# A pooling mixer on one core: S4 x B22 of the second input phase as seven inner products, its sums loaded, its stores on GpSimd's queue

## The chip, the core and the metric

The kernel runs on one core of a Trainium2 chip. Its engines work side by side, each through its own list of instructions in order, and wait for each other by semaphores: TensorE (PE: matmuls, with PEld for the loading of their stationary operand), VectorE (DVE), ScalarE (ACT), GpSimd (POOL) and SyncE (SP, which here only issues DMAs). A DMA that GpSimd issues runs in the software queue, one that SyncE issues in a hardware queue. The metric is the time of one execution on the device in microseconds (us). Three runs of the kernel before took 910.66, 911.06 and 911.10 us; the median is 911.06.

## The reference

The input x has 4096 rows (time) of 1024 channels. One layer of a pooling mixer is applied, with a norm before and a norm after:

```python
normed = rms_norm(x, norm_w)
u, gate = split(normed @ in_w, 2)               # in_w is 1024 x 2048
pooled[g] = trailing_mean(u[g], w_g) - u[g]     # 4 groups of 256 channels, w = 2, 4, 8, 16
mixed[g]  = pooled[g] @ group_w[g] + group_b[g]
y = mixed * scale * silu(gate)
out = rms_norm(x + y @ out_w, final_norm_w)
```

All of it is float32. What costs matmul time are the two large products, with in_w and with out_w.

## The kernel before, in words

**Precision.** Each operand of a matmul is split into a high part and a low part (`split`: ScalarE copies the high part, L165, VectorE subtracts for the low part, L159). A product is three matmuls: high x high, high x low, low x high.

**Weights.** group_w is multiplied into the u half of in_w at the start, so that an input product gives at once what is to be pooled.

**Stages.** The input product is made in two phases, a and b (`q` = 0 and 1), one for each two of the four groups: of its 1024 output columns, 512 are the gate and 512 are u. Each phase goes over NB = 4 blocks of 1024 rows. Then the output phase o goes over 8 blocks of 512 rows. In the trace, phase a runs from 33.8 to 324.7 us, the blocks of phase b begin at 324.7, 397.3, 469.8 and 542.3, and the output phase begins at 614.9 us.

**One block of an input phase.** It is a 2 x 2 block product by Winograd's form of Strassen's method, seven products in place of eight. A are the rows (split in two halves of time and two halves of channels), B the weights, C the result: C11 and C21 are gates, C12 and C22 are u. The products come in the order P1, P2, P7, P6, P5, P4, P3 (`ORDER_IN`), and each is one step:

- P1 = A11 B11, P2 = A12 B21, P4 = A22 by a combination of B;
- P7 takes S3 = A11 - A21, P6 takes S2 = A22 - S3, P5 takes S1 = A11 + S2;
- P3 = S4 B22 with S4 = A12 - S2; it is the last one, and completes C12.

A step is 48 matmuls (2 halves of channels x 4 tiles of columns x 2 x 3 passes) of a 128 x 128 stationary weight tile against 512 rows (`mm3`, L603). P1, P2, P7 and P4 collect in PSUM banks 0 to 3 (called x and v), P6, P5 and P3 in banks 4 to 7 (y). The sums of products are made by not clearing a bank between products, and by copying or adding banks on the way out (`evict_in`): P1's banks are copied to y; P2's go through Silu to C11 tiles; P6's and P7's are copied to tiles; P5's and P4's are added to those (L1033); P3's are copied.

**Sums.** In phase a, the operands A are read from a transposed x, normalized and summed (`form_in`), and the operands of P1, P2, P7 and P4 are also stored to DRAM (`sd`) through GpSimd's queue. Phase b loads those four back (`load_saved`, L532) and makes S2, S1 and S4 again (`form_in`, `form_s4`): six VectorE subtractions or additions of 128 x 1024 per block.

**Tiles.** Operands and results live in eleven `st` and eight `vt` tiles of 128 x 1024 floats, given out first in, first out (`Slots`): a tile comes free when its last reader is done, a store to DRAM among them. The split operands live in four `op` tiles, used in turn.

**Pooling.** When C21/C22 or C12/C11 are complete, `pool` makes the windowed sums on VectorE, multiplies by the gate, and stores the result to DRAM (`yd`, L792) by SyncE. `pool_later` says how many steps after its product this comes.

**Out weights.** In blocks 1 and 2 of phase b, after P5, `make_wo` loads rows of out_w, scales them on ScalarE (L246), combines them and stores the seven combinations (`wod`); block 3 loads and splits them (`load_w`).

**The output phase** multiplies what was stored in `yd` with these weights, again by seven products. From its third block on one of them, P2, is itself made as seven smaller products ("inner products", L701) with matmuls of 256 columns; their weights lie in four `st` tiles taken out of the turn (`kept`).

**Order.** The loop at the end of the kernel goes over all steps. At step n it issues the loads of the steps up to n + 3 (`load_reach`; n + 4 in phase o), the splits of step n + 1, the sums of step n + 2, the pooling that is due, and the product itself. A scheduler then orders each engine's instructions by these places in the program, except where `issue_after` holds an instruction behind a named one or `high_priority` moves it ahead. SyncE's queue and GpSimd's queue are in order: a DMA that waits holds up those behind it.

Of the kernel before, what the change touches and what calls it, by code (L numbers as in the profile page):

```python
# [15 lines left out]
P = 128  # L16
D = 1024
# [18 lines left out]
class Slots:  # L36
# [4 lines left out]
    def __init__(self, tiles):  # L41
        self.free = deque((0, t) for t in tiles)
        self.used = {}

# [9 lines left out]
    def keep(self):  # L54

        return self.renew(self.free.popleft()[1])

# [7 lines left out]
def kernel(  # L65
# [54 lines left out]

    def renew(t):
        i = next(i for i, u in enumerate(sts) if u is t)
        return mem.tile([P, D], F32R, tag=f"st{i}", name=f"inner{i}")

    st.renew = renew
# [41 lines left out]
    def split(dst, src):  # L167
# [17 lines left out]
        for i in range(P1, P7 + 1)  # L185
# [4 lines left out]
            for i in (P1, P2, P7, P4)  # L190
# [75 lines left out]
    def store_weights(dst, h, b11, b21, b12, b22):  # L266
        nc.sync.dma_start(out=dst[P1][h], in_=b11)
        nc.sync.dma_start(out=dst[P2][h], in_=b21)
        for i, u in combine(b11, b21, b12, b22).items():
            nc.sync.dma_start(out=dst[i][h], in_=u)  # L270
            give(u)

# [15 lines left out]

    def save_t3():

        for h in range(2):
            us = []
            for k in (h, 2 + h):
                us.append(take())
                nc.sync.dma_start(out=us[-1], in_=wvd[k])
            with tc.issue_after(evicted[0]):
                sub(us[0], us[1], us[0])
            nc.sync.dma_start(out=t3d[h], in_=us[0])
            for u in us:
                give(u)  # L300
# [22 lines left out]
    def split_wb(i):  # L323
        for h in range(2):
# [7 lines left out]
            if i != P6:  # L332
                give(u)

    def make_wo(h):
        us = {}
        for n in range(2):
            for kh in range(2):
                us[kh, n] = load_rows(out_w, 4 * kh + 2 * h, n * H)
                scale_rows(us[kh, n], pair(scale_c, h, kh))  # L340
        store_weights(wod, h, us[0, 0], us[1, 0], us[0, 1], us[1, 1])

    def load_w(src, i):
        for h in range(2):
            u = take()
            nc.sync.dma_start(out=u, in_=src[i][h])
            split(w[i][h], u)
            give(u)
# [187 lines left out]
    def load_in(q, b, i):  # L536
        s = xs[b]
        if i == P1:
            s["11"] = load_saved(b, P1) if q else load_x(b, 0, 0)
        elif i == P2:  # L540
            s["12"] = load_saved(b, P2) if q else load_x(b, 0, 1)
        elif i == P7:
            s["21"] = load_saved(b, P7) if q else load_x(b, 1, 0)
        elif i == P6:
            s["22"] = load_saved(b, P4) if q else load_x(b, 1, 1)

    def form_in(q, b, i):

        s = xs[b]
        if i in (P1, P2):  # L550
            if q == 0:
                for u in s["11" if i == P1 else "12"]:
                    normalize(b, 0, u)
        elif i == P7:
            if q == 0:
                for h in range(2):
                    normalize(b, 1, s["21"][h])
                    sub(s["21"][h], s["11"][h], s["21"][h])
        elif i == P6:
            s["2"] = [take(pool=early if (q, b) == (0, 0) else None) for _ in range(2)]  # L560
            for h in range(2):
                if q == 0:
                    normalize(b, 1, s["22"][h])
# [3 lines left out]
            if q == 0:  # L567
                give(rstd.pop(b))
        elif i == P5:
            for h in range(2):  # L570
                add(s["11"][h], s["2"][h], s["11"][h])
            if (q, b) != (0, 0):
# [3 lines left out]
    def split_in(q, b, i):  # L576
        s = xs[b]
        key = {P1: "11", P2: "12", P6: "2", P7: "21", P5: "11", P4: "22", P3: "12"}[i]
        later = q == 0 and b == 0 and i in (P1, P2)
        t = split_halves(s[key], None if q or later else sd[b].get(i))  # L580
        if later:
            stores.extend(zip(sd[0][i], s[key]))
        if i == P6 and (q or b):
# [24 lines left out]

# [839 lines left out]
```

## Time and profile before

| | before |
|---|---|
| median of three runs | 911.06 us |
| the profiled execution | 911.84 us |
| its span | 909.7 us |
| granted TensorE clock, mean | 0.997 |
| TensorE busy | 900.6 us (99%) |
| VectorE busy | 764.5 us (84%) |
| ScalarE busy | 461.8 us (51%) |
| moved by DMA | 178.08 MB, 196 GB/s on average |

The span goes from the first to the last instruction of the profiled execution; the 2.1 us beside it lie around it. Busy time is the time in which an engine had an instruction under way. Rows of groups read: line, engine, operation, written tile <- read tiles, shapes, x count | busy us, mean ns of one | idle time of the engine ahead of them <- what ended it. Rows of waits read: engine, line and who was waited for: us in total, times, longest. Rows of the chain read: start, us, what, count. Rows of DMA issues read: tiles, queue, count, KB each, us from issue to landing (the median).

### The profile page before, as it was taken

Reading aid. Unit: us, or ns where it says so; the run is one execution under the profiler, and the core shown is the slowest. Engines: PE = TensorE matmul, PEld = TensorE weight load, DVE = VectorE, ACT = ScalarE, POOL = GpSimd, SP = SyncE. Lnnn points to the kernel's source line nnn. Section 1 sums busy time; section 2 is a strip of 40 time slices with the busy share of each in tenths; the row PEclk is TensorE's granted clock in tenths of the full one; section 3 lists DMA queues with packets and bytes.
Section 4 is the critical chain, followed back from the end, with each engine's and each line's share of the span. In section 5 each row is a group of like instructions: output and inputs, shape, how many; then the busy total and the mean of one; then the engine's idle time right before and its main releaser. Section 6 shows DMA issues by size and latency. Waiting matters only on the chain.

```text
span 909.7 us, 11455 instructions
## 1 busy us (share of the span) xinstructions
PE 900.6 (99%) x4320; PEld 790.1 (87%) x4320; DVE 764.5 (84%) x909; ACT 461.8 (51%) x693; POOL 49.9 (5%) x124
## 2 busy tenths in 40 slices
PE   9999999999999999999999999999999999999997
PEld 7888888888888888888888888888888898888886
DVE  3889995985995997696798699699989878978886
ACT  7869547547446565355445545644424424335334
POOL 0020100100110000000000000000201001001000
PEclk9999999999999999999999999999999999999998
DMA  9977766577675454116616714636385464464332
GB/s 341 401 291 240 276 235 230 189 270 253 217 272 196 156 202 145 47 64 212 255 47 234 275 70 158 235 105 219 137 280 181 149 226 155 146 232 139 116 139 93
DMA packets 66807, 178.08 MB, mean 196 GB/s; under 512 B 6080, under 2 KB 23872, under 8 KB 66752
## 3 DMA queue, kind: packets, MB, share of 16 engines
q1 hardware_dynamic: 60176, 155.83, 48.8%
q0 software_dynamic: 5856, 20.46, 6.1%
q10 hardware_dynamic: 720, 1.06, 0.3%
q8 instruction: 34, 0.56, 0.2%
q14 instruction: 21, 0.17, 0.1%
HBM read 116.50 MB, written 60.83 MB: 195 GB/s over the span
## 4 chain that ended last, share of the span: by engine, by line
PE 91%; DMA 4%; DVE 3%; issue 1%; ACT 0%; SPq 0%; POOL 0%; DVEq 0%; ACTq 0%; POOLq 0%
PE bank L603 88%; PE bank L701 3%; DMA early<-in_wut 2%; DMA st<-in_x 1%; DMA vt<-yd 1%; DVE vt L1033 1%; PE bank L406 1%; DVE op L159 1%; DVE st L159 0%; DVE vt L916 0%; ACT st L943 0%; DVE vt L162 0%; DVE vt L711 0%; SPq L370 0%; DVE st L1033 0%
## 5 line engine op out<-in xcount | busy, mean ns | idle before, releaser
L603 PE MATMUL bank<-op,w 128*128 128x512 f32 x2688 | 580.9, 379 | 0.0
L603 PEld LDWEIGHTS bank<-op,w 128*128 128x128 f32 x2688 | 508.5, 189 | 71.8 <-ACT bank L165 0.4
L603 PE MATMUL bank<-w,op 128*128 128x512 f32 (+1 forms) x1212 | 262.2, 377 | 0.0
L603 PEld LDWEIGHTS bank<-w,op 128*128 128x128 f32 x1212 | 226.3, 189 | 30.7
L165 ACT ACTIVATE op<-st 128x1024 fp32r<-128x1024 f32 x129 | 134.7, 1053 | 142.2 <-PE bank L603 90.5
L159 DVE TENSOR_TENSOR op<-st,op 128x1024 fp32r<-128x1024 f32 x129 | 156.8, 1222 | 51.7 <-ACT op L165 51.3
L156 DVE TENSOR_TENSOR vt<-vt 128x1024 f32<-128x1024 f32 (+6 forms) x72 | 88.2, 1236 | 0.6
L159 DVE TENSOR_TENSOR op<-vt,op 128x1024 fp32r<-128x1024 f32 x43 | 52.5, 1222 | 19.8 <-ACT op L165 19.6
L165 ACT ACTIVATE vt<-bank 128x512 f32<-128x512 f32 x82 | 47.6, 593 | 41.4 <-PE bank L603 40.5
L165 ACT ACTIVATE op<-vt 128x1024 fp32r<-128x1024 f32 x43 | 45.1, 1053 | 39.3 <-PE bank L603 30.2
L159 DVE TENSOR_TENSOR st<-st,st 128x1024 f32<-128x1024 f32 (+1 forms) x43 | 47.0, 1111 | 2.3 <-ACT st L912 1.3
L165 ACT ACTIVATE bank<-bank 128x512 f32<-128x512 f32 x48 | 27.9, 581 | 32.9 <-PE bank L603 32.9
L1033 DVE TENSOR_TENSOR vt<-bank,vt 128x512 f32<-128x512 f32 (+1 forms) x55 | 37.1, 677 | 7.4 <-PE bank L603 7.0
L165 ACT ACTIVATE st<-bank 128x512 f32<-128x512 f32 x48 | 27.8, 593 | 28.7 <-PE bank L603 22.3
L207 POOL TENSOR_SCALAR oms<-oss 128x2 f32<-128x2 f32 x14 | 8.4, 601 | 565.5 <-ACT st L912 460.6
L159 DVE TENSOR_TENSOR w<-st,w 128x1024 fp32r<-128x1024 f32 x25 | 30.2, 1223 | 7.8 <-ACT w L165 7.8
L165 ACT ACTIVATE w<-st 128x1024 fp32r<-128x1024 f32 x25 | 26.0, 1052 | 14.2 <-PE bank L603 9.6
L788 DVE SCALAR_TENSOR_TENSOR st<-vt,colt,st 128x512 f32<-128x512 f32 x46 | 32.7, 752 | 0.1
L1033 DVE TENSOR_TENSOR st<-bank,st 128x512 f32<-128x512 f32 x42 | 28.8, 692 | 3.9 <-PE bank L603 3.7
L783 DVE SCALAR_TENSOR_TENSOR vt<-vt,vt 128x1024 f32<-128x1024 f32 x24 | 29.4, 1227 | 0.3
L916 DVE SCALAR_TENSOR_TENSOR vt<-vt,ors,st 128x1024 f32<-128x1024 f32 x18 | 22.5, 1282 | 7.9 <-POOL ors L225 7.9
L165 ACT ACTIVATE st<-st 128x1024 f32<-128x1024 f32 x16 | 16.9, 1059 | 21.8 <-DVE st L156 21.7
(132 smaller groups left out, 619.0 us busy)
## 6 DMA issues: line engine op xcount, KB each, us to landing
st<-in_x SPq DMA_DIRECT2D x30, 512.0 KB, 5.3
st<-in_xt SPq DMA_DIRECT2D x28, 512.0 KB, 5.6
sd<-st POOLq DMA_DIRECT2D x28, 512.0 KB, 4.6
vt<-in_x SPq DMA_DIRECT2D x27, 512.0 KB, 4.5
st<-sd SPq DMA_DIRECT2D x24, 512.0 KB, 4.2
yd<-st SPq DMA_DIRECT2D x23, 512.0 KB, 2.6
st<-yd SPq DMA_DIRECT2D x20, 512.0 KB, 4.6
out<-vt SPq DMA_DIRECT2D x18, 512.0 KB, 3.6
```

Source lines behind the costliest of these rows:

```text
L156: nc.vector.tensor_tensor(out=dst, in0=a, in1=b, op=ALU.add)
L159: return nc.vector.tensor_tensor(out=dst, in0=a, in1=b, op=ALU.subtract)
L165: return nc.scalar.activation(dst, src, func)
L207: (nc.vector if on_vector and not first else nc.gpsimd).tensor_scalar(out=ms, in0=ss, scalar1=1.0 / D, scalar2=EPS, op0=ALU.mult, op1=ALU.add)
L406: latest[0] = nc.tensor.matmul(ps, a[:, kk, 2 * j + t, :], maps, start=t + m == 0, stop=t == 1 and m == len(pairs) - 1,).ins
L603: latest[0] = nc.tensor.matmul(ps, a, b, start=start and n == 0, stop=stop and n == 2, skip_group_check=True).ins
L701: latest[0] = nc.tensor.matmul(ps, x1, x2, start=i in (P1, P7) and k + n == 0, stop=k == 1 and n == 2, skip_group_check=True,).ins
L783: nc.vector.scalar_tensor_tensor(out=s[:, :, at : at + H], in0=s[:, :, at : at + H], scalar=1.0 / win, in1=v[:, :, HIST:], op0=ALU.mult, o ...
L788: nc.vector.scalar_tensor_tensor(out=sg[:, j], in0=s[:, j, at : at + H], scalar=bias_c[2 * grp + j], in1=sg[:, j], op0=ALU.add, op1=ALU.mult,)
L916: nc.vector.scalar_tensor_tensor(out=us[j], in0=us[j], scalar=rs[:, j : j + 1], in1=fw[0], op0=ALU.mult, op1=ALU.mult,)
L1033: partial["added"] = nc.vector.tensor_tensor(out=dst, in0=src, in1=dst, op=ALU.add).ins
```

## The change

In phase b, for its blocks 0, 1 and 2 (`inner_at`):

1. P3 is made as seven inner products by the same method (`inner_in`): S4 and B22 are cut in 2 x 2 again, and each inner product is 12 matmuls with 256 columns, 84 in place of 48. Four half sums of S4 are made on VectorE and split (`split_inner_in`, `split_sums`); bank "one" is copied to "six" and "six" to "five" on ScalarE; VectorE adds the banks into the result (`to_rows`). The splits of the next step are issued in the middle of it (`then`).
2. The sums and low parts of the inner weights are made once, in block 0 (`form_inner_in`), and lie until the end of block 2 in four `st` tiles lent out of the turn (`lend`, `end`).

In both phases, for all blocks:

3. Phase a stores the operands of all seven products, phase b loads them all, and its `form_in` is gone.
4. In phase b the `yd` stores, and all `wod` stores, are issued by GpSimd in place of SyncE. `make_wo` is spread over three steps (load at P2, scale at P7, combine and store at P6); the loads and splits of the out weights in block 3 are two calls in place of one.
5. Most loads of phase b are issued two steps ahead in place of three. The splits of phase b from block 1 on have high priority. C21's and C22's pooling comes two steps after P4 where P3 is inner, and the Silu of C21 comes at the end of the inner step.
6. The raw operands of the t3 weights are loaded one step ahead of their subtraction, in block 3 of phase a in place of block 2.

```diff
+    def lend(self):
+
+        t = self.free.popleft()[1]
+        self.lent.append(self.index_of(t))
+        return self.renew(t)
+
+    def end(self):
+        for i in self.lent:
+            Slots.clock += 1
+            self.free.append((Slots.clock, self.revert(i)))
...
-            for i in (P1, P2, P7, P4)
+            for i in ORDER_IN
...
+        elif stage == 1:
+            with tc.issue_after(latest_copy[0]):
+                for (kh, n), u in wo_rows.items():
+                    scale_rows(u, pair(scale_c, h, kh))
+            nc.gpsimd.dma_start(out=wod[P1][h], in_=wo_rows[0, 0])
+            nc.gpsimd.dma_start(out=wod[P2][h], in_=wo_rows[1, 0])
+        else:
+            b11, b12, b21, b22 = (wo_rows.pop((kh, n)) for kh in range(2) for n in range(2))
+            with tc.issue_after(latest_split[0]):
+                us = combine(b11, b21, b12, b22)
+            for i, u in us.items():
+                nc.gpsimd.dma_start(out=wod[i][h], in_=u)
...
+        if q:
+            s[i] = load_saved(b, i)
...
+        if q:
+            t = split_halves(s[i])
+            if i == P3 and inner_at(b):
+                t = split_inner_in(t, s[i])
+            for u in s.pop(i):
+                give(u)
+            return t
...
+    def inner_at(b):
+        return b < NB - 1
...
+            sub(t3, b22, b12)
+            add(t2, t3, b11)
+            sub(t1, b22, t2)
+            sub(t4, b21, t2)
...
+        hi, lo = (st.lend().rearrange(pattern, **sizes) for _ in range(2))
+        copy(hi, r)
+        sub(lo, r, hi.bitcast(F32))
+        give(r)
...
+        (a11, a21), (a12, a22) = ([quarter(u, g) for g in range(2)] for u in us)
+        vs = [take("p (n k s a) -> p n k s a", n=2, k=2, s=2) for _ in range(2)]
+        (s4, s2), (s3, s1) = ([v[:, n] for n in range(2)] for v in vs)
+        sub(s3, a11, a21)
+        sub(s2, a22, s3)
+        sub(s4, a12, s2)
+        add(s1, s2, a11)
...
+        o = next_op("p (x n k s a) -> p x n k s a", x=2, n=2, k=2, s=2)
+        split(o, v)
+        give(v)
...
+            for ct in range(2):
+                bank, g = (y[place[0] + ct], place[1]) if place else (spare, ct)
+                ps = bank.rearrange("p (a s) -> p a s", s=2)[:, g * P : (g + 1) * P]
+                for k in range(2):
+                    lt = [v[:, k, ct * P : (ct + 1) * P] for v in b]
+                    r = [v[:, k].rearrange("p s a -> p a s") for v in t[i]]
+                    for n, (x1, x2) in enumerate(((lt[0], r[0]), (lt[0], r[1]), (lt[1], r[0]))):
+                        latest[0] = nc.tensor.matmul(
+                            ps, x1, x2, start=i in (P1, P7) and ct + k + n == 0,
+                            stop=k == 1 and n == 2, skip_group_check=True,
+                        ).ins
...
+        def to_rows(bank, *places):
+            src = bank.rearrange("p (c a s) -> p c s a", c=2, s=2)
+            for g, n in places:
+                dst = rows[n][:, :, HIST:].rearrange("p c (s a) -> p c s a", s=2)
+                dst = dst[:, :, :, g * P : (g + 1) * P]
+                add(dst, src, dst)
+
+        go(P1)
+        copy(six, one)
+        go(P2)
+        go(P4)
+        go(P6)
+        copied_on = copy(five, six).ins
+        then()
+        go(P3)
+        for c, dst in enumerate(cells(rows, HIST)):
+            with tc.issue_after(copied_on):
+                evicted[0] = copy(halved(dst), plain(y[c])).ins
+        to_rows(one, (0, 0))
+        to_rows(six, (1, 0))
+        go(P7)
+        to_rows(seven, (1, 0), (1, 1))
+        go(P5)
+        to_rows(five, (0, 1), (1, 1))
...
-            nc.sync.dma_start(
+            (nc.gpsimd if q else nc.sync).dma_start(
...
-            with tc.issue_after(evicted[0]) if i == P6 else nullcontext():
+            with ExitStack() as order:
+                if i == P6:
+                    order.enter_context(tc.issue_after(evicted[0]))
+                if kind == "b" and b:
+                    order.enter_context(tc.high_priority())
                 split_up[n] = split_in(kind == "b", b, i)
...
-            wait = int(b == 0) if kind == "a" else 1 if b < NB - 1 else 2
+            wait = int(b == 0) if kind == "a" else 2 if inner_at(b) else 1
...
+        early_one = b == 0 and i in (P1, P2, P7) or b == NB - 1 and i != P1
+        return 2 if kind == "b" and not early_one else 3
...
+        inside = kind == "b" and i == P3 and inner_at(b)
+        if inside:
+            for half in range(2):
+                split_sums(split_up[n], half)
+        else:
+            due()
```

More of the change, by code (lines that the diff above doesn't have):

```diff
@@ L804, in cells, with gates @@
         return [us[c // 2][:, c % 2, lo:] for c in range(4)]
+    def gates(us):
+        for u in us:
+            copy(u, u, AF.Silu)
     def evict_in(b, q, i, sets, seeds=4):
```

205 lines of the change are left out of this document (134 added, 71 removed).

## The prediction

> **What bounds the kernel now.** I read the page first (busy shares), then TensorE's waits, the chain that ended last, the engines by stretches, and last the groups by shape.
>
> ```profile
> span 909.7 us, 11455 instructions
> PE 900.6 (99%) x4320; PEld 790.1 (87%) x4320; DVE 764.5 (84%) x909; ACT 461.8 (51%) x693; POOL 49.9 (5%) x124
> PE bank L406 <- DMA early<-in_wut: 1.0, 3, 0.4
> PE bank L1135 <- PEq L1433: 0.8, 1, 0.8
> PE bank L406 <- DMA early<-in_group_w: 0.4, 1, 0.4
> PE bank L701 <- DVE vt L711: 0.3, 1, 0.3
> ```
>
> TensorE is busy for 99% of the span, and its whole list of waits is 2.5 us long: three rows of the first 30 us and 0.3 us late in the output phase. So the kernel lasts as long as its matmuls last, and an edit counts in two ways only: by the matmul time that it takes away, and by the waits that it puts between matmuls. Neither another engine's load nor a transfer's length is a term by itself.
>
> ```profile
> 47.57 655.54 PE bank L603 x3036
> 703.11 3.35 PE bank L701 x30
> 709.05 0.73 PE bank L701 x6
> 712.37 0.67 PE bank L701 x6
> 738.94 3.35 PE bank L701 x30
> ```
>
> In the chain, 3036 matmuls of 512 columns follow each other in 655.54 us: 215.9 ns each. The output phase already holds matmuls of 256 columns (L701, the same strided reading of the moving side, the same three passes); 30 take 3.35 us: 111.7 ns each. One stretch of six is at 121.7 ns (0.73 us), the next at 111.7.
>
> ```profile
> 252.20:324.70 72.50, 72.50 (x338) 63.56 (x337) 61.55 (x66) 37.79 (x55) 2.13 (x4) 1.00 0.59 201
> 324.70:397.30 72.60, 72.60 (x338) 63.65 (x337) 59.98 (x66) 34.68 (x47) 0.00 (x0) 1.00 0.33 115
> 397.30:469.80 72.50, 72.50 (x337) 63.56 (x337) 59.52 (x59) 34.54 (x52) 0.00 (x0) 1.00 0.45 167
> 469.80:542.30 72.50, 72.50 (x337) 63.56 (x337) 59.39 (x59) 34.37 (x52) 0.00 (x0) 1.00 0.51 182
> ```
>
> Columns: stretch, its length, then busy time of PE, PEld, DVE, ACT and POOL, clock, DMA share, GB/s. Rows 2 to 4 are blocks 0 to 2 of the second input phase. One is 72.5 us long, seven products of 10.36 us; the clock is full, VectorE has some 12.5 us free in it, ScalarE 38, the DMA engines half of their time. That is the room into which the change puts its work.
>
> **The sum, part by part.**
>
> *Inner products.* In three blocks P3 (48 matmuls of 512 columns) becomes seven products of 2 x 2 x 3 = 12 matmuls of 256: 84. 48 x 215.9 = 10.36 us, 84 x 111.7 = 9.38 us: 0.98 us less per block, 2.93 in all. The dear stretch (121.7 ns) would make it 10.22 us, 0.14 us less per block, 0.4 in all. I take 111.7, which both long stretches show. The Trainium skill ("TensorE: Matmul & The Clock Gate", section "Wait — 56ns, not 53.3ns?") gives a warm matmul its columns at 2.4 GHz and about 2.5 ns beside; as an estimate that is 109.2 ns for 256 columns, 9.17 us for 84, and 3.6 us less in all. The trace agrees at 512 columns and stands 2.5 ns above at 256, so the trace's figure decides.
>
> ```profile
> L159 DVE TENSOR_TENSOR op<-st,op 128x1024 fp32r<-128x1024 f32 x129 | 156.8, 1222 | 51.7 <-ACT op L165 51.3
> L165 ACT ACTIVATE op<-st 128x1024 fp32r<-128x1024 f32 x129 | 134.7, 1053 | 142.2 <-PE bank L603 90.5 <-DVE st L159 18.8 <-PE bank L701 11.3
> L159 DVE TENSOR_TENSOR st<-st,st 128x1024 f32<-128x1024 f32 x37 | 44.5, 1222 | 2.2 <-ACT st L912 1.3 <-ACT st L246 0.6 <-DMA st<-wvd 0.2
> L1033 DVE TENSOR_TENSOR vt<-bank,vt 128x512 f32<-128x512 f32 x53 | 36.2, 687 | 7.4 <-PE bank L603 7.0
> L165 ACT ACTIVATE bank<-bank 128x512 f32<-128x512 f32 x48 | 27.9, 581 | 32.9 <-PE bank L603 32.9
> ```
>
> *VectorE and ScalarE.* An inner block adds on VectorE four sums of half size (no such row; the nearest, 128x512 out of a bank, is 687 ns: 2.7 us), two low parts (1222: 2.4) and six adds out of the banks (687: 4.1): 9.3 us. The loaded sums take away form_in's six adds (1222: 7.3). Net +2.0 on 59.5, and block 0 pays another 5.2 once for the inner weights (4 x 0.69 + 2 x 1.22): 67.2 of 71.5 us at most, so not the bound. ScalarE gets two op copies (1053) and two bank copies (581) more: +3.3 on 34.5. Throughput costs nothing here; order can.
>
> *Order inside the inner step.* T is the end of P4, and the step lasts 9.38 us. By the instruction order and these durations, the copy of bank one to bank six, which P6 needs at T + 4.0 (36 matmuls after T), is done at T + 3.2; the copy of six to five, needed at T + 8.0, at T + 6.2; the next block's first operands, needed at T + 9.4, at T + 6.5. P4's last bank is drained by T + 0.8, and nothing writes there before. The thinnest slack is 0.8 us: no cost taken, 0.5 us per block as the other end.
>
> *Splits at higher priority.* They come earlier in both queues, not later. What stands behind them waits instead: pooling and gates, due a step or more later. Cost 0.
>
> ```profile
> SPq L792 <- DVE st L788: 168.6, 23, 21.0
> SPq L792 <- DVE vt L788: 46.6, 9, 11.1
> sd<-st POOLq DMA_DIRECT2D x28, 512.0 KB, 4.6
> st<-sd SPq DMA_DIRECT2D x24, 512.0 KB, 4.2
> yd<-st SPq DMA_DIRECT2D x23, 512.0 KB, 2.6
> st<-in_out_w SPq DMA_DIRECT2D x6, 512.0 KB, 5.3
> L515 POOL DMA_DIRECT2D sd<-st x25 | 13.4, 537 | 88.1 <-DVE tmp L162 36.3 <-DVE st L159 22.5 <-DVE st L162 18.9
> ```
>
> *Stores through GpSimd's queue.* Today SyncE stands for 215 us in front of yd stores (first two rows), and the loads behind a store wait with it. In the second phase these stores and the wod stores go to GpSimd, 0.54 us per issue on an engine that did nothing there. SyncE is freed, but the tile under a store comes free later (landing 4.6 us on GpSimd against 2.6 on SyncE), and a store may now stand behind another's wait on GpSimd. The Trainium skill ("DMA: Bandwidth & Descriptors", section "Anatomy of one DMA — SWDGE (gpsimd) path") gives such a DMA 2.0 us plus its bytes at 436 GB/s; for 512 KB that is an estimate of 3.2 us, 0.6 more than on SyncE, which the slacks below would take; by the trace's 4.6 it is 2.0 more, which they would not everywhere, and the trace decides. The price is in the tightest place, below.
>
> *Loads and saved sums.* 24 more stores in phase a and 24 more loads in b, 512 KB each: 3.1 MB per block on 14.6 (201 GB/s x 72.5 us) and on 8.3 to 13.2 MB; by the same rows the DMA share rises to about 0.72 in a3 and to 0.45 to 0.63 in b. The four tiles lent to the inner weights leave seven of eleven for b0 to b2, so a load there waits more often for a store.
>
> ```profile
> 33.80:107.10 73.30, 73.30 (x344) 64.08 (x344) 65.11 (x85) 56.67 (x87) 11.10 (x21) 1.00 0.78 290
> 69.00:72.00 3.00, 3.00 (x15) 2.63 (x15) 3.00 (x4) 3.00 (x5) 0.00 (x0) 1.00 1.02 418
> 72.00:75.00 3.00, 3.00 (x16) 2.63 (x15) 3.00 (x4) 3.00 (x7) 0.00 (x0) 1.00 0.22 86
> 74.48 0.57 ACT L165 ACTIVATE st<-bank 128x512 f32<-128x512 f32 x1
> 76.57 1.55 ACT L165 ACTIVATE st<-bank 128x512 f32<-128x512 f32 x3
> ```
>
> *Block 0 of phase a.* DMA is full (share 1.02) until 72 us, and the new P5 store is issued into that, by my count at about 66 us; ScalarE's eviction of 74.48 us now waits for its tile until the store has landed. P5 starts three steps before the block's end, at 76.0; its second bank is needed six matmuls later, at 77.3, and was free at 77.1 (the first of three evictions from 76.57). Landing between 70 and 75 us gives 0 to 1 us of waiting; I take 0.1.
>
> *The tightest place: block 1 of b, from P6 to P5.* u is the block's start, 397.3 in the trace of before.
>
> ```profile
> 434.31 1.04 ACT L165 ACTIVATE op<-st 128x1024 fp32r<-128x1024 f32 x1
> 436.38 0.60 ACT L165 ACTIVATE st<-bank 128x512 f32<-128x512 f32 x1 [0.54 <-PE bank L603]
> 438.97 0.60 ACT L165 ACTIVATE st<-bank 128x512 f32<-128x512 f32 x1 [0.70 <-PE bank L603]
> 439.46 1.05 ACT L165 ACTIVATE op<-st 128x1024 fp32r<-128x1024 f32 x1
> DMA to landing us min/median/max: 3.1/4.2/7.7
> DMA to landing us min/median/max: 2.9/3.8/10.2
> ```
>
> Before, P6's second bank was evicted at 436.38, ahead of P4's operand copies (439.46 on). In the changed order P4's first operand copy stands between the evictions of the first and the second bank, so a late load holds up the evictions, and P5 writes those banks. That load waits in SyncE's queue behind one whose tile comes free with P5's second low part (about u + 35.4 by my count of VectorE), and for a yd store on GpSimd that stands behind a wod store, which waits for a scaling, for a load of out_w and for the store before it. Issue at u + 36, landing at u + 40.2 (4.2 us: the first of the two landing rows, for loads of sd on SyncE in b), copy until 41.2, eviction until 41.8; P5 needs the bank at u + 42.7 (41.4 plus six matmuls). Slack 0.9 us. At 7.7 us the wait is 2.6. If the store at the chain's head lands like the slowest of sd on GpSimd (10.2, second landing row, 105 to 330 us) and not at 4.6, it is 4.7. I take 0, nearest to the medians; ends 0 and 4.7. In block 2 the same copy is ready at about u + 38, ahead of need.
>
> *Elsewhere.* The out weights in three stages, t3's loads ahead of their use and the later gates are the same instructions at other steps, 6 to 10 us from their users; where they stand in a queue ahead of a load is counted above. Cost 0. The output phase and the tail keep their order: 0 ± 0.3 us.
>
> Sum: -2.93 + 0.1 = -2.8 us. The profiled execution took 911.84 us, 2.1 beside its span; it would become 909.0. It stands 0.8 above the median of the runs, 911.06, so the median becomes **908.2 us**. Ends without the large waits: 907.5 (2.93, 0.4 for the scatter of the runs shown, 910.66 to 911.1, and 0.2 in the tail) to 909.2 (1 us of waits).
>
> **The rivals.**
>
> *Late operand in b1 (the opposite side).* For it: the order above, the long rows of SyncE's waits, seven tiles in place of eleven. Against: 0.9 us of slack at median landings, and DMA at 0.45 before. One landing of 7.7 us gives 2.6 - 2.8: 910.9 us, within 0.2%. From 4.7 us of wait on (the load lands 5.6 us later than I count) the kernel is slower by over 0.2%; that is 913.0, and with both stores of the chain at 10.2 (11.2 late, 10.3 of wait) 918.6.
>
> *The weights bound the small matmuls.*
>
> ```profile
> L701 PEld LDWEIGHTS bank<-inner,op 128*128 128x128 f32 x144 | 18.7, 192 | 1.6 <-DVE vt L711 1.1
> ```
>
> A weight load shows 192 ns, and 84 of them in a row would be 16.1 us, 5.8 more than P3 now in each block: 928.4 us. Against it stand the 30 matmuls in 3.35 us, which have a load each.
>
> *Phase a pays.* Where DMA is full the new stores push each other back. If the eviction of 74.48 comes at 77, P5 waits 2 us: 910.2 us, within 0.2%. Against: the share drops to 0.22 from 72 us on.
>
> *It does not shorten.* If the copy of one to six came 1.8 us later than I count in each block (0.8 of slack, then the 0.98), the saving would be spent: 911.1. Against: the output phase's own inner products (L701) wait 0.3 us in all.
>
> **How the numbers follow.** 0.2% (1.8 us) is about what a measurement of this kernel can tell from no change: 909.2 and 912.9 are the bounds. Forecast 0.64 (faster). Late operand 0.24: 0.12 small, 0.12 decisive. Phase a 0.06, no shortening 0.04 (both within). Weights 0.02. So faster 0.64, same 0.22, slower 0.14. The range leaves out the decisive late operand and the weights above (0.14) and about 0.05 below: 907.2 to 912.9. The forecast's own is 907.5 to 909.2.
>
> **What would show it.** Right: P3's steps of 9.4 us in b0 to b2, TensorE with no wait between 31 us and the output phase, matmuls of 256 columns at 112 ns, VectorE's busy time up by about 4 us over b (11.2 more, 7.3 less in b3), yd rows gone from SyncE's waits. Wrong: a wait of TensorE on a bank that ScalarE evicts, at P5 of b1 or of a0, with a load of sd as the copy's releaser; or 256-column stretches above 120 ns.

## The result, and the profile after

The changed kernel takes 924.11 us (median of six runs, 921.53 to 928.53) against 911.08 us before: a ratio of 1.0145, with a 95% interval of 1.0121 to 1.0168. It is 13 us slower, where 2.9 us faster was forecast. The profiled execution took 923.97 us, 12.1 us more than the profiled one before.

The page of the changed kernel, and the four longest of TensorE's waits:

```profile
span 922.2 us, 11888 instructions
PE 902.6 (98%) x4428; PEld 792.9 (86%) x4428; DVE 768.2 (83%) x927; ACT 469.1 (51%) x707; POOL 69.3 (8%) x176
PE bank L647 <- DVE op L177: 5.0, 2, 4.3
PE bank L731 <- DVE st L174: 3.4, 2, 2.6
PE bank L647 <- ACT st L183: 1.5, 2, 1.3
PE bank L647 <- DVE st L1196: 1.0, 1, 1.0
```

Four rows that were not there before hold 10.9 us, nearly all on VectorE. Where they lie shows the timeline of TensorE's matmuls (start, length, what, and in brackets the wait ahead of it; L731 is the inner product of phase b, L647 the old L603, L858 the old L701). The changed kernel:

```profile
386.63 2.84 PE L731 MATMUL bank<-op,w 128*128 128x256 f32 x24
396.00 42.90 PE L647 MATMUL bank<-op,w 128*128 128x512 f32 x198
440.23 19.69 PE L647 MATMUL bank<-op,w 128*128 128x512 f32 x90 [1.32 <-ACT st L183]
460.71 2.92 PE L731 MATMUL bank<-op,w 128*128 128x256 f32 x24 [0.79 <-DVE st L174]
470.17 62.33 PE L647 MATMUL bank<-op,w 128*128 128x512 f32 x288
535.11 4.35 PE L731 MATMUL bank<-op,w 128*128 128x256 f32 x24 [2.62 <-DVE st L174]
546.00 72.69 PE L647 MATMUL bank<-op,w 128*128 128x512 f32 x336
618.52 11.20 PE L647 MATMUL bank<-w,op 128*128 128x512 f32 x50
630.39 20.56 PE L647 MATMUL bank<-w,op 128*128 128x512 f32 x94 [0.67 <-DVE op L177]
651.99 11.59 PE L647 MATMUL bank<-w,op 128*128 128x512 f32 x51 [1.04 <-DVE st L1196]
667.92 47.87 PE L647 MATMUL bank<-w,op 128*128 128x512 f32 x213 [4.34 <-DVE op L177]
715.62 1.50 PE L858 MATMUL bank<-w,op 128*128 128x256 f32 x12
```

The same view of the kernel before:

```profile
614.89 88.22 PE L603 MATMUL bank<-w,op 128*128 128x512 f32 x408
702.95 1.50 PE L701 MATMUL bank<-w,op 128*128 128x256 f32 x12
```

With the block ends of before (397.3, 469.8, 542.3, 614.9) the distance between the two kernels at each boundary is:

| boundary | before | after | after - before |
|---|---|---|---|
| end of b0 | 397.3 | 396.0 | -1.3 |
| end of b1 | 469.8 | 470.2 | +0.4 |
| end of b2 | 542.3 | 546.0 | +3.7 |
| end of b3 | 614.9 | 618.5 | +3.6 |
| first inner product of the output phase | 702.95 | 715.62 | +12.7 |
| end of the span | 909.7 | 922.2 | +12.5 |

So block 0 gains, blocks 1 and 2 lose 1.7 and 3.3 us, and the first two output blocks, which the change hardly touches, lose 9 us.

What TensorE waited for in block 2, on VectorE, in the list of DMA issues and in GpSimd's timeline of the changed kernel:

```profile
524.29 0.69 DVE L177 TENSOR_TENSOR vt<-vt 128x512 f32<-128x512 f32 x1 [8.06 <-DMA wod<-vt]
wod<-vt POOLq DMA_DIRECT2D x10, 512.0 KB, 7.4
515.51 0.53 POOL L370 DMA_DIRECT2D wod<-vt  x1 [1.74 <-DVE vt L177]
```

The half sums of S4 are written to a `vt` tile whose last reader is a wod store. GpSimd issued it at 515.51; it landed 8.7 us later. VectorE stood still for 8.06 us, came late to the draining of P4's banks, and the first inner product waited 2.62 us for those.

In block 1 it was P4's operand, as the prediction's tightest place has it (1.32 us), and then the same draining (0.79 us), here behind a yd store on GpSimd: it was issued at 434.72 and landed 7.3 us later, SyncE's queue stood for it, and the loads of P3's operand went out only at 442.02. ScalarE's copy and VectorE's half sums came late behind them:

```profile
434.72 0.53 POOL L949 DMA_DIRECT2D yd<-st  x1 [4.43 <-DVE st L945]
448.42 1.06 ACT L183 ACTIVATE op<-st 128x1024 fp32r<-128x1024 f32 x1 [7.27 <-DMA st<-sd]
449.51 1.23 DVE L177 TENSOR_TENSOR op<-st,op 128x1024 fp32r<-128x1024 f32 x1 [8.56 <-ACT op L183]
```

The stretches around the output phase's beginning, columns as in the prediction (busy time of PE, PEld, DVE, ACT, POOL; clock, DMA share, GB/s); first before, its first two output blocks, then the changed kernel, its blocks 0 and 3 of phase b and the first output block:

```profile
614.90:650.00 35.10, 35.10 (x164) 30.78 (x163) 35.10 (x40) 9.67 (x13) 0.00 (x0) 1.00 0.53 182
650.00:686.00 36.00, 36.00 (x169) 31.55 (x168) 32.78 (x40) 18.46 (x28) 7.39 (x11) 1.00 0.62 218
```

```profile
324.80:396.00 71.20, 71.20 (x372) 63.50 (x371) 50.32 (x56) 37.83 (x52) 0.00 (x0) 1.00 0.40 140
546.00:618.50 72.50, 72.50 (x338) 63.51 (x337) 68.17 (x70) 39.66 (x56) 2.13 (x4) 1.00 0.63 212
618.50:655.50 37.00, 35.29 (x161) 30.00 (x160) 37.00 (x39) 9.59 (x11) 1.59 (x3) 1.00 0.50 155
```

Already before, VectorE was busy for 35.10 of the first output block's 35.10 us. Work that comes late into that stage can't be made up there. In the changed kernel block 0 has 9.7 us of VectorE's work less than before (50.32 against 59.98), block 3 has 4.0 more (68.17 against 64.18) although it lost 7.3 us of `form_in`, the sums that are now loaded.

One price was in no sum. After its two longest waits TensorE runs for some 3 us at half its clock (the value behind PE, PEld, DVE, ACT and POOL; stretches of the changed kernel):

```profile
532.00:535.10 3.10, 0.49 (x3) 0.10 (x2) 1.96 (x3) 1.81 (x4) 0.00 (x0) 0.94 0.00 0
535.10:538.10 3.00, 2.99 (x14) 3.00 (x15) 2.79 (x4) 0.53 (x2) 0.00 (x0) 0.50 0.00 0
667.90:671.00 3.10, 3.08 (x7) 2.52 (x8) 3.10 (x3) 0.00 (x0) 0.00 (x0) 0.50 0.98 342
```

The 24 matmuls at 535.11 took 4.35 us in place of 2.84, so the wait of 2.62 cost 1.5 more. Behind the wait of 1.32 us (440.23) 90 matmuls took 19.69 us, 219 ns each: no such loss.

### The profile page after: what moved, and what is told of

The parts are those of the page before. It is cut to its first block, busy times and chain, and to the rows that moved or that the text cites. A ratio compares the mean times of both kernels' runs of the same rounds, so it can differ in the third digit from the quotient of the medians.

```text
span 922.2 us, 11888 instructions
## 1 busy us (share of the span) xinstructions
PE 902.6 (98%) x4428; PEld 792.9 (86%) x4428; DVE 768.2 (83%) x927; ACT 469.1 (51%) x707; POOL 69.3 (8%) x176
## 5 line engine op out<-in xcount | busy, mean ns | idle before, releaser
L647 PE MATMUL bank<-op,w 128*128 128x512 f32 x2544 | 550.9, 379 | 1.5 <-ACT st L183 1.5
L647 PEld LDWEIGHTS bank<-op,w 128*128 128x128 f32 x2544 | 480.2, 189 | 70.7 <-ACT st L183 2.5
L647 PE MATMUL bank<-w,op 128*128 128x512 f32 (+1 forms) x1212 | 265.1, 379 | 6.1 <-DVE op L177 5.0
L647 PEld LDWEIGHTS bank<-w,op 128*128 128x128 f32 x1212 | 226.8, 190 | 39.2 <-DVE op L177 5.8
L177 DVE TENSOR_TENSOR op<-st,op 128x1024 fp32r<-128x1024 f32 x112 | 135.7, 1219 | 51.7 <-ACT op L183 51.3
L183 ACT ACTIVATE op<-st 128x1024 fp32r<-128x1024 f32 x112 | 117.0, 1053 | 116.0 <-PE bank L647 45.7
L183 ACT ACTIVATE op<-vt 128x1024 fp32r<-128x1024 f32 x66 | 69.2, 1055 | 78.0 <-PE bank L647 42.8
L177 DVE TENSOR_TENSOR op<-vt,op 128x1024 fp32r<-128x1024 f32 x66 | 80.1, 1218 | 13.3 <-ACT op L183 13.0
L174 DVE TENSOR_TENSOR vt<-bank,vt 128x512 f32<-128x512 f32 (+1 forms) x57 | 36.1, 677 | 3.8 <-ACT vt L183 2.0
L1196 DVE TENSOR_TENSOR vt<-bank,vt 128x512 f32<-128x512 f32 (+1 forms) x43 | 28.8, 670 | 6.6 <-PE bank L647 6.5
L551 POOL DMA_DIRECT2D sd<-st x38 | 20.3, 534 | 129.1 <-DVE tmp L180 35.1
L180 DVE TENSOR_TENSOR st<-st,vt 128x1024 f32<-128x1024 f32 x22 | 26.1, 1215 | 3.4 <-DMA vt<-rd 3.4
L1079 DVE SCALAR_TENSOR_TENSOR st<-st,ors,st 128x1024 f32<-128x1024 f32 x16 | 20.1, 1281 | 6.8 <-POOL ors L243 6.8
```

What stands on the lines that cost most here:

```text
L174: nc.vector.tensor_tensor(out=dst, in0=a, in1=b, op=ALU.add)
L177: return nc.vector.tensor_tensor(out=dst, in0=a, in1=b, op=ALU.subtract)
L180: nc.vector.tensor_tensor(out=dst, in0=a, in1=b, op=ALU.mult)
L183: return nc.scalar.activation(dst, src, func)
L551: first_saves.append(nc.gpsimd.dma_start(out=saved[h], in_=u).ins)
L647: latest[0] = nc.tensor.matmul(ps, a, b, start=start and n == 0, stop=stop and n == 2, skip_group_check=True).ins
```

## The experiments

All times are medians; each ratio is to the kernel before on the same chip, with its 95% interval. On the chips used the kernel before took 911.1 to 911.6 us, so times from two chips compare to about half a us. Waits are read from one profiled execution each; such an execution can lie up to 4.6 us from the median (e17). Theory A: the stores on GpSimd's queue hold tiles too long. Theory B: the inner products with seven tiles are too tight by themselves. After the first four runs came C (pooling one step later leaves VectorE behind at the output phase), D (the four tiles that the output phase keeps back, the `kept` tiles, taken half a block earlier than before, from P5 of output block 0 on; the list of the change ahead leaves this edit out) and E (out weights split one step later).

### Who issues the stores, and the inner products left out

```diff
 # e1: both edits; e2: only the second (three places)
-            (nc.gpsimd if q else nc.sync).dma_start(
+            nc.sync.dma_start(
-            nc.gpsimd.dma_start(out=wod[P1][h], in_=wo_rows[0, 0])
+            nc.sync.dma_start(out=wod[P1][h], in_=wo_rows[0, 0])
```

> The changed kernel with the yd and wod stores of the second phase issued by SyncE again; all else as changed. Theory A (the stores on GpSimd's queue land late, 5.8 us for wod and 4.8 for yd at the median, and the tiles under them hold up what takes them next: the inner half sums in block 2 waited 8.1 us for a wod store) expects VectorE's 8.1 us wait to go, TensorE's waits in phase b and in the output phase to fall from 12 to under 3 us, and 908 to 911 us. Theory B (seven tiles in place of eleven and the inner work are too tight by themselves, whoever issues the stores) expects waits of the same size in other places and 918 us or more.

Measured: 918.7 us, 1.0080 (1.0064 to 1.0097). TensorE's timeline:

```profile
388.84 2.84 PE L731 MATMUL bank<-op,w 128*128 128x256 f32 x24
460.38 2.84 PE L731 MATMUL bank<-op,w 128*128 128x256 f32 x24
531.92 2.84 PE L731 MATMUL bank<-op,w 128*128 128x256 f32 x24
664.60 47.93 PE L647 MATMUL bank<-w,op 128*128 128x512 f32 x213 [4.26 <-DVE op L177]
```

The inner steps now begin 71.54 us apart, where a block took 72.5: 0.97 us less, just the matmuls' saving, and no wait in phase b. So A is right for phase b: with the stores on SyncE the change earns its 2.9 us there. But the 4.3 us wait in the second output block stays (4.26). The forecast of A, 908 to 911, is missed by 8 us, and something else must cause that wait. The time is as B forecast (918 or more), but not at B's place: phase b has no wait with its seven tiles.

> The changed kernel with only the wod stores issued by SyncE again; yd stores stay on GpSimd. If the wod stores are the part of theory A that counts (block 2's 8.1 us wait, and the work of VectorE that it pushes into the output phase), 911 to 915 us, with the 4.3 us wait in the output phase gone. If the yd stores count as much, or theory B holds, 918 us or more.

Measured: 919.86 us, 1.0089 (1.0072 to 1.0105). The 8 us wait of VectorE is gone, and of TensorE's waits in phase b 1.0 us is left. The 4.34 us wait is still there, so it doesn't come from block 2's stall, against the expectation. The wod stores alone are 4.2 of the 5.4 us between the changed kernel and the one with all its stores on SyncE.

```diff
 # e3
     def inner_at(b):
-        return b < NB - 1
+        return False
```

> The changed kernel without the inner products: P3 is 48 matmuls in all blocks, no inner weights, no lent tiles; sums are still loaded, stores still on GpSimd, splits still at high priority. Theory A expects that it stays slow: 916 us or more (2.9 us of matmul time come back, and the late stores stay). Theory B expects 909 to 912 us: no wait of TensorE in phase b and none over 1 us in the output phase.

Measured: 914.21 us, 1.0032 (1.0020 to 1.0044), between the two expectations. Without inner products, but with stores on GpSimd, phase b has no wait, and the 4.3 us are gone; a wait of 2.08 us comes later, at 708 us. The inner products, which save 2.9 us of matmuls, cost 9.9 us in the changed kernel (924.11 less 914.21), together with what the edit takes out beside them: the four lent tiles and the pooling two steps after P4.

> The kernel before with one part alone: yd stores of the second phase and all wod stores on GpSimd's queue. Theory A expects 914 us or more, from tiles that come free late. Theory B expects 911 us, within 1 us, since eleven tiles give the stores time to land.

Measured: 913.03 us, 1.0019 (1.0010 to 1.0028), between the two expectations. Its edit is the same change of queue, made to the kernel before. One wait comes of it, and it lowers the clock behind it as well:

```profile
496.38 122.39 PE L603 MATMUL bank<-op,w 128*128 128x512 f32 x558 [2.00 <-ACT vt L165]
496.30:499.40 3.10, 3.02 (x8) 2.51 (x9) 2.09 (x2) 1.93 (x3) 0.48 (x1) 0.60 0.87 262
```

So the queue alone costs 1.5 us with eleven tiles and six adds per block, and 5.4 us in the changed kernel. A holds in kind, though less than it forecast.

### The wait in the second output block

In the run with the stores on SyncE, the operand that comes late at 664.60 is loaded by SyncE like this:

```profile
646.81 0.32 SPq L949 DMA_DIRECT2D yd<-st  x1
647.18 0.43 SPq L1012 DMA_DIRECT2D vt<-yd  x1
```

The load stands right behind a yd store, which waits for block 3's last pooling on VectorE. In the changed kernel the same load is issued at 650.12, when that pooling frees its tile. Both lead to VectorE's pooling and to the tiles; each of the next four runs is meant to take away one suspect. All are the kernel with its stores on SyncE (918.7 us) and one more edit.

```diff
 # e5: inner products in blocks 0 and 1
-        return b < NB - 1
+        return b < NB - 2
```

> The stores on SyncE (918.7 us), and the inner products in blocks 0 and 1 only, so that block 2's P4 half is pooled one step after P4 as before. Theory C (pooling one step later moves one half's pooling, about 14 us of VectorE, out of each block into the next, and the last one's into block 3 and the output phase, where VectorE has no room) expects the 6 us of TensorE's waits at 624 to 665 us to fall under 2 us: 910 to 912 us, 1 us of matmul time more included. Theory D (the four tiles kept back from output block 0 on, in place of block 1, make its loads late) and theory E (the out weights, split one step later, are late) expect 917 to 920 us.

Measured: 913.70 us, 1.0018 (1.0007 to 1.0029), between the expectations of C and of D and E. The wait fell from 4.3 to 1.63 us:

```profile
656.98 46.46 PE L647 MATMUL bank<-w,op 128*128 128x512 f32 x214 [1.63 <-DVE op L177]
```

Its runs stand in two groups, 911.1 to 911.3 (three, the profiled one among them) and 912.5 to 915.0 (seven). In the profiled one the clock held after a wait of 1.63 us. The mean granted clocks go with the groups: 0.998 to 0.999 in the three, 0.996 to 0.997 in six of the seven. That the clock fell behind this wait in those is likely, but no trace of them shows it.

```diff
 # e6: block 2's P4 half is not pooled
+            cut = q == 1 and b == 2 and half == 1
-            if win == 2:
+            if cut:
+                pass
+            elif win == 2:
...
-            for j in range(2):
+            for j in range(0 if cut else 2):
```

> The stores on SyncE (918.7 us), three blocks with inner products, and for block 2's P4 half the windowed sums, the mean and the product with the gate left out (the gate itself is stored): 7 adds of 1.24 us, 2 means of 1.22 and 4 products of 0.75, 14.2 us of VectorE less, at the same steps and with the same tiles and stores. Theory C expects the waits in the output phase under 2 us and 908 to 911 us. Theories D and E expect 916 us or more, since the tiles and weights come as before.

Measured: 911.82 us, 1.0004 (0.9994 to 1.0014). With 14.2 us of VectorE's work less the load goes out at 641.22 us in place of 647.18, the wait is 2.29 us (in a profiled execution of 914.33 us), and the kernel is as fast as before, though not faster; C's range is missed by 0.8 us, its limit for the wait by 0.3. VectorE's lateness is one cause; a wait remains that it doesn't explain.

```diff
 # e7: the tiles kept back as before
-        if kind == "o" and b < 2 and not inner_w and (b or i in (P5, P4, P3)):
+        if kind == "o" and b == 1 and len(kept) < 4 and not inner_w:
...
-            if len(kept) == 4 and b:
+            if len(kept) == 4:
```

> The stores on SyncE (918.7 us), and the four tiles of the output phase's inner weights kept back from output block 1 on, as in the kernel before. Theory D expects the 4.3 us wait at 664 us to go: 911 to 914 us. Theories C and E expect 917 to 920 us.

Measured: 913.32 us, 1.0022 (1.0013 to 1.0032), as D expected. In place of the long wait there are 1.04 and 0.61 us, and 0.88 us later, in the third output block. The fourth load of yd in the output phase, which went out at 647.18, goes out ahead of the store that waits for the pooling:

```profile
629.79 0.37 SPq L1012 DMA_DIRECT2D st<-yd  x1
```

> The stores on SyncE (918.7 us), and the out weights loaded and split in one call in block 3, as in the kernel before. Theory E expects the waits of 1.4 and 0.7 us at 626 us and the 4.3 us at 664 us to go: 910 to 913 us. Theories C and D expect 917 to 920 us, with at most the 2 us at 626 us gone.

Its edit calls load and split of the out weights together after each product of block 3, as the kernel before does. Measured: 915.78 us, 1.0044 (1.0029 to 1.0059). The waits near 626 us are 1.8 us in place of 2.0; the long one is 3.1, with 0.7 ahead of it. E is the smaller part: 2.9 of 7.2 us.

So the load is late because four tiles are missing (D) and because the pooling is late that would give others back. Taking away either one takes 5 to 7 us of the 7.2 by which that kernel stood above the one before (918.70 against 911.55). That the pooling is late because it comes one step later, as C has it, is not shown: e5 also takes block 2's inner work away and ends the loan of the four tiles a block earlier, and e6 leaves work out altogether.

### Together, and each alone

> The stores on SyncE, three blocks with inner products, and both small restorations together: four tiles kept back from output block 1 on, out weights loaded and split in one call. If the two act on different waits, their gains add: 918.7 - 5.4 - 2.9 = 910.4 us. If both only make room for the same late pooling (theory C), 912 to 914 us, with waits of TensorE on VectorE left in the output phase.

Measured (edits of e7 and e8 together): 912.96 us, 1.0016 (1.0006 to 1.0026). The gains don't add. TensorE's list of waits:

```profile
PE bank L654 <- DVE st L1203: 1.8, 1, 1.8
PE bank L654 <- DVE op L177: 1.5, 1, 1.5
PE bank L865 <- DVE vt L875: 0.9, 1, 0.9
```

4.2 us, all on VectorE, all in the first three output blocks. That is nearly the balance: the median is 1.8 us above before, and the matmuls save 2.9, which makes 4.7.

> The same two restorations with the yd and wod stores on GpSimd's queue, as in the change. If the stores' price (5.4 us between the changed kernel and the one with its stores on SyncE) is paid in blocks 1 and 2, by tiles that come free late, it stays: 4 to 7 us above the run with the stores on SyncE, and VectorE's wait for a wod store in block 2 is there. If it was paid through the output phase, within 1.5 us of that run.

Measured: 927.05 us, 1.0168 (1.0138 to 1.0197), 14.1 us above the run before it, which differs only in who issues the stores. Block 2's stall is there, 8.5 us of VectorE waiting for a wod store, and in the first output block one more wait, of TensorE (in a profiled execution of 922.81 us):

```profile
DVE vt L177 <- DMA wod<-vt: 8.5, 1, 8.5
631.40 1.15 PE L654 MATMUL bank<-w,op 128*128 128x512 f32 x2 [5.00 <-ACT op L183]
```

The expectation for a price paid in blocks 1 and 2 (4 to 7 us) is exceeded; the stall is carried on to where VectorE has no room, and grows there.

> The stores on SyncE, inner products in blocks 0 and 1 only, out weights loaded and split in one call. Theory C with the late weights as a second load on VectorE: 910 to 912.5 us, the 1.6 us wait at 657 us gone. If only the tiles count there (theory D), 913.7 us as without it, within 1 us.

Measured: 913.82 us, 1.0033 (1.0021 to 1.0046): no better than with two inner blocks alone (913.70), as theory D expected. Two waits of 1.6 us on VectorE, at 627 and 660 us.

> The stores on SyncE, inner products in blocks 0 and 1 only (913.7 us), and the splits of phase b without high priority. If the priority is what keeps the splits ahead of the pooling, TensorE waits in blocks 1 and 2 for split operands: 916 us or more. If it only reorders VectorE's work, within 1 us of 913.7.

Its edit takes the high priority away. Measured: 914.54 us, 1.0034 (1.0025 to 1.0044), 0.8 us above the run with it, where the two intervals overlap. One wait of 0.60 us in phase b: the priority is worth little either way.

> The changed kernel with inner products in blocks 0 and 1 only; stores on GpSimd and all else as changed. If pooling one step later in block 2 is what fills VectorE before the output phase, and block 2's half sums are what waits for the wod store, both go: 913 to 917 us, and VectorE's 8 us wait for a wod store is gone. If the stores on GpSimd cost as much without it, 920 us or more.

Measured: 917.78 us, 1.0066 (1.0046 to 1.0085). On the changed kernel itself, too, block 2 without inner products takes 6.3 us away. VectorE's 8 us wait for a wod store is gone, as expected (one of 0.8 us is left); waits of 2.53 us in block 1 and 1.50 in block 3 for evictions by ScalarE remain, and 1.33 and 2.38 us on VectorE in the output phase. The expected range is missed by 0.8 us.

> Three blocks with inner products and both restorations (912.96 us), with the yd stores of block 3 alone on GpSimd's queue. If what is left in the output phase comes from loads that stand behind those stores in SyncE's queue, 910 to 912 us and the waits at 625 and 708 us shorter. If it comes from VectorE's work alone, within 1 us of 913.

Its edit issues the yd stores of block 3 alone through GpSimd. Measured: 913.14 us, 1.0017 (1.0007 to 1.0027), with the same three waits (2.0, 1.2 and 0.9 us). So what is left doesn't come from block 3's stores in SyncE's queue; VectorE's work is the cause that fits.

> Stores on SyncE, inner products in blocks 0 and 1, the four tiles kept back from output block 1 on (with one free tile left over in place of two, without which they are not there in time). If the pooling and the tiles were the two causes in the output phase, both are gone: 909 to 911 us. If VectorE is still behind there, 913 to 914 us as with each alone.

Measured: 914.00 us, 1.0036 (1.0023 to 1.0048). Both causes reduced, and no gain: 1.45, 0.90 and 1.95 us of waits on VectorE, the last at 810 us. Neither expectation named that place.

> The changed kernel without inner products and with all stores on SyncE: what is left are the loaded sums, the splits at high priority, the out weights in stages and the tiles kept early. If the sums' extra traffic costs nothing and the rest is harmless without the inner products, 911 to 912 us. If the loaded sums cost by themselves, 913 us or more.

Measured: 915.40 us, 1.0046 (1.0031 to 1.0061). Phase b runs without a wait, so the loaded sums cost nothing there. But the late load is back, without any inner product and with block 2's pooling one step after P4 as before (in a profiled execution of 920.02 us, 4.6 above the median):

```profile
663.37 49.05 PE L645 MATMUL bank<-w,op 128*128 128x512 f32 x214 [4.56 <-DVE op L177]
```

With the stores on GpSimd and no inner products (914.21) it wasn't there: then the load doesn't stand behind the store, and goes out at 638.16 in place of 645.95. So SyncE's order is a cause as well, where tiles are kept back early. The same trace shows a part of theory E: VectorE stands idle for 3.37 us (until 632.60) for ScalarE's copy of the last out weights, whose load went out at 625.44, against 612.04 in the kernel before. So the wait doesn't need the inner products. What makes e17 4.2 us longer than before, where the early keeping alone makes 1.6 (e19, next), was not separated further. Moving the stores takes this wait away (914.21 against 915.40 us, whose intervals overlap), and harms phase b (e1, e4).

```diff
 # e18 and e19: the kernel before, with
-        if kind == "o" and b == 1 and len(kept) < 4 and not inner_w:
+        if kind == "o" and b < 2 and not inner_w and (b or i in (P5, P4, P3)):
 # e18 alone, besides
-            wait = int(b == 0) if kind == "a" else 1 if b < NB - 1 else 2
+            wait = int(b == 0) if kind == "a" else 2 if b < NB - 1 else 1
```

> The kernel before with one small part alone: the four tiles kept back from output block 0 on. If theory D holds by itself, 913 to 916 us with a wait of TensorE near 660 us on an operand whose load came late; if the tiles matter only where VectorE is behind, 911 us within 1 us.

Measured: 912.98 us, 1.0018 (1.0008 to 1.0027). The load of yd that goes out at 629.56 in the kernel before goes out at 643.28, right behind a yd store.

> The kernel before with two small parts of the change: P4's half is pooled two steps after P4 in blocks 0 to 2 and one step after it in block 3, and the four tiles of the output phase's inner weights are kept back from output block 0 on. If the pooling costs by itself (theory C), 2 to 6 us above the run with the tiles alone, with waits of TensorE on VectorE in the output phase; if it needs the inner products' extra work to matter, within 1 us of that run.

Measured: 912.77 us, 1.0019 (1.0010 to 1.0029). The wait at the same place, in e19 and in e18:

```profile
659.49 48.14 PE L603 MATMUL bank<-w,op 128*128 128x512 f32 x214 [2.11 <-DVE op L159]
```

```profile
658.23 46.46 PE L603 MATMUL bank<-w,op 128*128 128x512 f32 x214 [1.55 <-DVE op L159]
```

The early keeping costs 1.6 us by itself and makes this wait even in the kernel before; D holds alone. Pooling one step later adds nothing to it (0.2 us less). Whether C holds with the inner products' work beside it was not tried with the delay as the only difference.

No version was faster than the kernel before. What stays open: how the 5.4 us of the stores' price in the changed kernel divides between tiles and the clock, and whether the inner products pay if VectorE's work in the first output blocks is made smaller; e6, the only run at the level of before with three inner blocks, points that way but leaves pooling out.

## Why the prediction was wrong

- **The matmuls: right.** 84 in 9.37 us (386.63 to 396.00 us), forecast 9.38. With the stores on SyncE all three blocks show it.
- **"The tightest place": right place, wrong size.** The load went out at u + 37.5 (433.52 us) where I counted u + 36, and took 5.1 us, not 4.2. TensorE waited 1.32 us where I took 0; my other end was 4.7. It is the sign of being wrong that I had named.
- **"Order inside the inner step": right inside, wrong at its door.** Nothing waits within the three steps. But "P4's last bank is drained by T + 0.8" rested on VectorE being on time, and the half sums' own tile, under a wod store, was not followed. That store landed after 8.7 us, and block 1's yd store after 7.3, where I reckoned with 4.6 for one on GpSimd. The waits that came of them, 2.62 and 0.79 us, have no place in the prediction beyond its 0.5 us per block as the other end.
- **"Throughput costs nothing here": the step that failed most.** I compared VectorE's sum with each block of phase b, 67.2 of 71.5 us at most, and was right that it isn't the bound there: it was busy for 50.32, 61.16 and 60.58 us in blocks 0 to 2. But block 0's 67.2 was too high by 17 us, mostly since the later pooling takes some 14 us out of that block, and I didn't follow where they go. The first output block was not looked at, where VectorE was already full (35.10 of 35.10). Block 2's P4 half pooled later, block 3's pooling behind it, the split of the out weights one step later: each moves work into a stage without room. e6 shows it by leaving 14.2 us out: 6.9 us faster.
- **"Elsewhere ... 0 ± 0.3": wrong by 9 us.** I judged the output phase by its order, which is nearly the same. The edit of `kept`, three lines of the diff, was costed nowhere; it takes four tiles half a block earlier. Alone it costs 1.6 us (e19), in the changed kernel with its stores on SyncE 5.4 us (e7).
- **Splits at higher priority: cost 0, right** within what e12 can tell.
- **Loads and saved sums: the mean right, the peak missed.** The share of DMA in block 3 of phase a is 0.80 (0.72 forecast), in b 0.40 to 0.63 (0.45 to 0.63). In block 2, loads, yd and wod stores meet: 0.96 from 510 to 520 us, and there the 8.7 us landing falls. In block 0 of phase a P5 waited 0.20 us; I took 0.1.
- **The rivals.** "Late operand in b1" came at its small size (1.32 us of wait, less than the 2.6 us that it priced within 0.2%), and had a ceiling of 918.6 us. The real time lies above that for another reason: the late stores hold up blocks 1 and 2 by other ways too, and the output phase loses 9 us. So the 0.14 for slower, which rested on a decisive late operand and on the weights, is no merit of the prediction. That VectorE becomes the bound in a later stage was no rival at all.

## What to carry to other kernels

A busy share is a share of a stage: ask of every engine, in every stage behind the change, whether it is full there, for delayed work arrives in that stage and not in the one where it was made. Follow each tile taken from a first-in first-out turn back to its last reader, stores included, and follow the small edits of the allocation as closely as the large ones. Where two engines are near full, gains need not add: the restorations of e7 and e8, worth 5.4 and 2.9 us alone, gave 5.7 us together (e9).

## What the runs showed of the hardware

A wait of TensorE has a second price. After waits up to 1.80 us the granted clock stayed at 1.00; after 1.89, 2.00 and 2.11 us its mean was 0.68, 0.60 and 0.55 in the 3.1 us that followed (e12, e4, e19); after ten waits of 2.29 to 5.00 us it was 0.50 to 0.67. Three waits of 1.95, 1.98 and 2.08 us left it at 1.00 (e15, e14, e3). The lost time shows in the matmuls behind the wait: 213 or 214 of them took 47.87 to 49.05 us, against 46.46 for 214 where the clock held (e5, e18), and the 24 behind block 2's wait in the changed kernel took 4.35 in place of 2.84. So a fall cost 1.5 to 2.6 us; it cost most in e2 and e17, where the clock was at 0.50 for 5 us.

Near 2 us either outcome came up, and the traces don't show what decides it. The Trainium skill ("TensorE: Matmul & The Clock Gate", section "What's actually happening") tells of a free-running window of about 3.4 us and of an idle one that halves the clock. Two outcomes at nearly one length would fit a free-running window; that waits of 1.89 to 3.11 us, shorter than such a window, can be enough, these runs show and the page does not.
